# Decoder step: q, k and v of three token blocks in products of 512 columns, and modulation moved beside the RWKV inputs

## The chip, the core and the metric

The kernel runs on one core of a Trainium2 chip. The metric is the device time of one launch in microseconds, as a median over runs. TensorE multiplies, VectorE and ScalarE work on the elements, GpSimd does little here, and nearly all loads and stores are issued by SyncE, whose queue (SP) is taken in order.

## The reference

One layer of a decoder for a prompt of 2048 tokens and 64 sample tokens, all in fp32. Cut to what matters here:

```
sh1, sc1, gt1, sh2, sc2, gt2 = ada_modulation(c, w_ada, b_ada)   # silu(c) @ w_ada + b_ada, six parts of 1024
h = rms_norm(x, norm1_g) * (1.0 + sc1) + sh1
proj = h @ w_in                                                  # 1024 -> 3 * 512 (q, k, v) + 1792 (RWKV inputs P)
q, k = partial_rope(q), partial_rope(k)                          # 16 of each head's 64 elements turn
att = dilated attention of three branches over q, k, v
rw  = RWKV-7 time mixing over P (a recurrence over the tokens)
x = x + gt1 * (concat(att, rw) @ w_out)
h2 = rms_norm(x, norm2_g) * (1.0 + sc2) + sh2
x = x + gt2 * (square(relu(h2 @ w_ff1)) @ w_ff2)
y = rms_norm(x, normf_g)
```

k, v, the last row of P and the RWKV states are outputs too.

## The kernel before

The prompt is cut into four blocks of 512 tokens (0 to 3); block 3 also takes the 64 sample tokens. The tokens ORDER list the parts in the order in which they are written down, with a time span for each: i0 to i3 are the input projections (`in_stage`), r0 to r3 the RWKV recurrence, a0 to a3 the attention, s and c the sample tokens, m, p and f the output projection and the MLP. A scheduler then sets each engine's order from these times and its own costs, so parts overlap: RWKV of block 0 runs while blocks 0 to 2 are projected, and so on. All engines take their own list in order, so a row that waits holds back what stands behind it.

Every large product is done in three (`mm3`): operands are split into a high part and a rest (`split`: ScalarE writes the high part, VectorE the rest), and hi*hi, hi*lo and lo*hi are added in PSUM. `in_stage` of a block goes like this.

- For each of its token tiles (128 tokens; "tile 0" to "tile 3"): load x (name xt, two buffers), `norm_A` on ScalarE, then `norm_B`: eight transposes on TensorE in two groups of four (line 279, into PSUM tiles trps), eight scalings on VectorE (line 284, into h32, three buffers), split into hhi and hlo (lines 303, 304). hhi and hlo hold one block only, so these last two steps wait until the block before has been multiplied.
- Seven blocks of 256 weight columns for the RWKV inputs, block 6 first. Here the weights are stationary and the tokens stream, 512 columns a product (block 6 in two halves of 256 tokens). The result goes through pev to the DRAM scratch Pd.
- Six blocks of 256 weight columns for q, k and v. Here 128 tokens are stationary and 256 weight columns stream: 6 column blocks x 4 token tiles x 8 parts of the contraction x 3 = 576 products a block of tokens. Two token tiles share one PSUM bank; it is evicted by ScalarE (line 423, name qev, in two buffers of the tag pev), q and k are turned on VectorE, and the result goes to DRAM.

Weights come in two loads of 512 KB for each column block (name stg, two buffers), and the split halves go into w0 and w1 in turn. The modulation's parts 0 and 1 are made at the start. Parts 2 to 5 (`ada_rest`, a generator in S.bg) are made during block 1: before each of its 13 column blocks the generator takes three steps, a step being one load of 512 KB into stg and 32 small products (line 225) that add up in one PSUM bank.

PSUM has eight banks: two with the tag mm, for the large products; two with the tag tr, for the transposes of x and the modulation; four for RWKV and attention. Banks and buffers of a tag are handed out in the order in which the program is written.

Names in the rows: yps, zps, btps, vtps, aps, px, pu, psS, ops, lps are products and transposes of RWKV; qtps, s1ps, s2ps, ptps, pops of the attention; mps and wada the modulation.

Of the kernel before, what the change touches and what calls it, by code (L numbers as in the profile page):

```python
# [23 lines left out]
HD = 64  # L24
# [78 lines left out]
def run(gen, n):  # L103
    for _ in range(n):
        next(gen, None)
# [17 lines left out]
class Step:  # L123
# [184 lines left out]
        nc.scalar.activation(hi, h32[:, :, 0:rows], AF.Copy)  # L308
        nc.vector.tensor_tensor(lo, h32[:, :, 0:rows], hi.bitcast(F32), op=ALU.subtract)

    def mm3(self, out, wh, wl, xh, xl, nk):
        nc = self.nc
        self.tc.cur_priority += LEAD
        for k in range(nk):
            nc.tensor.matmul(out, wh(k), xh(k), start=k == 0, stop=False)  # L315
            nc.tensor.matmul(out, wh(k), xl(k), start=False, stop=False)  # L316
            nc.tensor.matmul(out, wl(k), xh(k), start=False, stop=k == nk - 1)  # L317
        self.tc.cur_priority -= LEAD

    def x_tile(self, j, X, norm=True):  # L320
# [6 lines left out]
    def w_in(self, c0, G):  # L327
        nc = self.nc
        tag = f"w{self.nwb % 2}"
        self.nwb += 1  # L330
        lo = G.tile([128, KD, 256], F32R, name="wlo", tag=tag)
        hi = G.tile([128, KD, 256], F32R, name="whi", tag=tag)
        for h in range(2):
            sl = slice(128 * h, 128 * h + 128)
            sg = G.tile([128, KD, 128], F32, name="stg", tag="stg")
            src = self.I["w_in"][0][:, c0 + 128 * h:c0 + 128 * h + 128]
            nc.sync.dma_start(sg, src.rearrange("(k p) c -> p k c", p=128))
            self.split(hi[:, :, sl], lo[:, :, sl], sg)
        return hi, lo

    def in_stage(self, s, G, psg, x0=(), first=None):
        nc, I, O = self.nc, self.I, self.O
# [26 lines left out]
            pend = new  # L369
        def wblock(c0):  # L370
            self.tick()
            w = first if first and c0 == 3 * ATT + 6 * 256 else self.w_in(c0, G)
            if self.bg is not None:
                run(self.bg, 3)
            return w

        for pb in (6, 0, 1, 2, 3, 4, 5):
            cols = self.halves(T) if last or pb == 6 else [(0, TS)]
            hi, lo = wblock(3 * ATT + pb * 256)
            evs = [G.tile([128, NW], F32, name="pev", tag="pev", bufs=2) for _ in range(2)]  # L380
            for c0, n in cols:
                for h in range(2):
# [19 lines left out]
        nc.sync.dma_start(rope[:, 0:4], I["rope"][t0:t0 + TS].rearrange("(j p) e -> p j e", p=128))  # L402
        if last:
            nc.sync.dma_start(rope[0:NS, 4], I["rope"][SEQ:SEQ + NS])
        for cb in range(6):
            hi, lo = wblock(cb * 256)
            kind, hh = cb // 2, (cb % 2) * 256
            for jp in range(3 if last else 2):
# [1077 lines left out]
def tile_hybrid_step(tc, I, O):  # L1486
# [76 lines left out]
    for tok in ORDER.split():  # L1563
# [5 lines left out]
        if tok[0] == "i":  # L1569
# [4 lines left out]
            if w == 0:  # L1574
                start.close()
                S.rwkv_setup()
                S.att_setup()
            if w == 1:
                full(S.bg)
                S.bg = None  # L1580
                S.A2, S.B2 = S.mod(3, 4, S.g2n, "A2")
# [111 lines left out]
```

## Time and profile before

| | |
|---|---|
| median of 3 runs | 3506.4 us (3504.91 to 3524.51) |
| the profiled execution | 3507.64 us, of which its span is 3505.8 us |
| TensorE busy | 3289.1 us, 94% of the span |
| weight loads of TensorE | 2794.4 us, 80% |
| VectorE, ScalarE busy | 2208.3 us (63%), 1709.7 us (49%) |
| mean granted TensorE clock | 0.965 |

A busy share counts a matmul from its start to the modelled end of its pipeline, so neighbours overlap, and a sum of matmul durations is more than the time they take. The time that a row of products needs is read from one start to the next. The profile has 40 slices of 87.6 us; the parts spoken of here lie in the first 960 us.

### The profile page before, as it was taken

The numbers are of one execution on the slowest core, as the hardware profiler recorded it, in microseconds if no ns is written. First come the engines' busy times: TensorE is split into PE (matmuls) and PEld (weight loads), VectorE is DVE, ScalarE is ACT, GpSimd is POOL, SyncE is SP. The second block draws the span as 40 slices with busy tenths as digits, with TensorE's granted clock in tenths as the row PEclk, the third lists the DMA queues.
The fourth block names the chain that finished last, engine by engine and source line by source line (L and its number), as shares of the span: only waits on it lengthen the run. The fifth ranks groups of instructions, "written<-read, shape, count | busy, mean of one in ns | idle before, by whom it ended". The sixth has DMA issues, their size and how long they took to land.

```text
span 3505.8 us, 66390 instructions
## 1 busy us (share of the span) xinstructions
PE 3289.1 (94%) x26546; PEld 2794.4 (80%) x26546; DVE 2208.3 (63%) x4872; ACT 1709.7 (49%) x3156; POOL 95.2 (3%) x219
## 2 busy tenths in 40 slices
PE   6999999888989999999999999799989998899998
PEld 4887888877878777878777777687767777899998
DVE  4565655625677566877766656675444877766666
ACT  4455444644355355546535442565333545544453
POOL 0000000000000000000000000000000000000000
PEclk8999999998989999999999999899999999899999
DMA  7456745434353443336344342843786335456564
GB/s 242 143 155 194 205 132 145 113 88 96 79 172 100 120 127 94 102 110 207 86 134 134 87 101 74 254 130 109 207 251 182 88 97 154 115 160 178 162 184 154
DMA packets 731757, 496.55 MB, mean 142 GB/s; under 512 B 126134, under 2 KB 682344, under 8 KB 731448
## 3 DMA queue, kind: packets, MB, share of 16 engines
q1 hardware_dynamic: 718824, 479.65, 47.6%
q0 software_dynamic: 12624, 12.65, 1.5%
q8 instruction: 210, 3.44, 0.4%
q14 instruction: 99, 0.81, 0.1%
HBM read 424.11 MB, written 63.77 MB: 139 GB/s over the span
## 4 chain that ended last, share of the span: by engine, by line
PE 79%; DMA 9%; ACT 5%; DVE 5%; issue 1%; SPq 0%; ACTq 0%; DVEq 0%
PE mmps L317 19%; PE mmps L315 19%; PE mmps L316 19%; PE pops L1047 2%; PE aps L652 2%; PE ptps L1057 2%; DMA out_dram<-pev 2%; DMA kst<-in_cache_k_dram 1%; DVE wl L259 1%; PE ktps L1231 1%; DMA stg<-in_w_out_dram 1%; DVE ql L951 1%; PE ops L794 1%; PE yps L729 1%; DMA wada<-in_w_ada_dram 1%
## 5 line engine op out<-in xcount | busy, mean ns | idle before, releaser
L258 ACT ACTIVATE wh<-stg 128x1024 fp32r<-128x1024 f32 x384 | 406.2, 1058 | 568.8 <-PE mmps L316 473.8
L315 PE MATMUL mmps<-h2hi,wh 128*128 128x256 f32 (+2 forms) x1864 | 628.4, 337 | 13.1 <-ACT h2hi L303 7.9
L317 PE MATMUL mmps<-h2hi,wl 128*128 128x256 f32 (+2 forms) x1864 | 628.7, 338 | 9.5 <-DVE wl L259 9.4
L259 DVE TENSOR_TENSOR wl<-stg,wh 128x1024 fp32r<-128x1024 f32 x384 | 469.9, 1225 | 260.3 <-ACT wh L258 240.9
L316 PE MATMUL mmps<-h2lo,wh 128*128 128x256 f32 (+2 forms) x1864 | 627.6, 337 | 1.0 <-DVE h2lo L304 1.0
L315 PE MATMUL mmps<-hid,wh 128*128 128x512 f32 (+2 forms) x1280 | 460.2, 361 | 5.6 <-ACT rlu L1419 3.8
L317 PE MATMUL mmps<-hid,wl 128*128 128x512 f32 (+2 forms) x1280 | 461.6, 361 | 0.1
L316 PE MATMUL mmps<-hid,wh 128*128 128x512 f32 (+2 forms) x1280 | 460.8, 360 | 0.0
L315 PEld LDWEIGHTS mmps<-h2hi,wh 128*128 128x128 f32 x1864 | 360.7, 194 | 44.5 <-ACT h2hi L303 8.8
L317 PEld LDWEIGHTS mmps<-h2hi,wl 128*128 128x128 f32 x1864 | 359.7, 193 | 41.2 <-DVE wl L259 12.0
L316 PEld LDWEIGHTS mmps<-h2lo,wh 128*128 128x128 f32 x1864 | 360.5, 193 | 30.0 <-issue 1.8
L315 PEld LDWEIGHTS mmps<-hid,wh 128*128 128x128 f32 x1280 | 243.5, 190 | 36.6 <-ACT rlu L1419 4.3
L317 PEld LDWEIGHTS mmps<-hid,wl 128*128 128x128 f32 x1280 | 243.7, 191 | 31.9 <-issue 3.4
L316 PEld LDWEIGHTS mmps<-hid,wh 128*128 128x128 f32 x1280 | 243.9, 191 | 29.4 <-issue 1.8
L1302 DVE SCALAR_TENSOR_TENSOR acc<-mmps,ada,acc 128x512 f32<-128x512 f32 (+1 forms) x280 | 179.3, 642 | 129.8 <-PE mmps L317 128.7
L315 PE MATMUL mmps<-whi,hhi 128*128 128x256 f32 (+1 forms) x816 | 233.8, 286 | 0.0
L317 PE MATMUL mmps<-whi,hlo 128*128 128x256 f32 (+1 forms) x816 | 233.1, 286 | 0.0
L316 PE MATMUL mmps<-wlo,hhi 128*128 128x256 f32 (+1 forms) x816 | 233.0, 286 | 0.0
L315 PE MATMUL mmps<-hhi,whi 128*128 128x512 f32 (+2 forms) x608 | 213.4, 353 | 13.5 <-ACT pev L393 6.9
L316 PE MATMUL mmps<-hlo,whi 128*128 128x512 f32 (+2 forms) x608 | 212.2, 350 | 1.1 <-DVE hlo L304 1.1
L317 PE MATMUL mmps<-hhi,wlo 128*128 128x512 f32 (+2 forms) x608 | 211.9, 349 | 0.0
L259 DVE TENSOR_TENSOR wlo<-stg,whi 128x1024 fp32r<-128x1024 f32 x104 | 126.6, 1228 | 90.9 <-ACT whi L258 90.5
(345 smaller groups left out, 5886.8 us busy)
## 6 DMA issues: line engine op xcount, KB each, us to landing
stg<-in_w_ff_dram SPq DMA_DIRECT2D x320, 512.0 KB
stg<-in_w_in_dram SPq DMA_DIRECT2D x104, 512.0 KB
stg<-in_w_out_dram SPq DMA_DIRECT2D x64, 512.0 KB
kst<-in_cache_k_dram SPq DMA_DIRECT2D x80, 256.0 KB
vst<-in_cache_v_dram SPq DMA_DIRECT2D x80, 256.0 KB
xt<-in_x_prompt_dram SPq DMA_DIRECT2D x32, 512.0 KB
wada<-in_w_ada_dram SPq DMA_DIRECT2D x32, 512.0 KB
Pd<-pev SPq DMA_DIRECT2D x56, 256.0 KB
```

Of the source, the lines that this page charges most:

```text
L258: nc.scalar.activation(hi, src, AF.Copy)
L259: nc.vector.tensor_tensor(lo, src, hi.bitcast(F32), op=ALU.subtract)
L315: nc.tensor.matmul(out, wh(k), xh(k), start=k == 0, stop=False)
L316: nc.tensor.matmul(out, wh(k), xl(k), start=False, stop=False)
L317: nc.tensor.matmul(out, wl(k), xh(k), start=False, stop=k == nk - 1)
L652: nc.tensor.matmul(pt[:, hp], bk[o:o + 64, hp, c], F[o:o + 64, hp, c], start=True, stop=True)
L729: nc.tensor.matmul(pz[q, u], x, y, start=True, stop=True, tile_position=(64 + o, 64 + o))
L794: nc.tensor.matmul(po[o:o + 64, h // 2, 64 * c:64 * c + 64], UV[0:64, c, h], AO[:, unit(h)], start=False, stop=c == 1 and h >= 6, tile_pos ...
L951: nc.vector.tensor_tensor(lo, pv[o], hi.bitcast(F32), op=ALU.subtract)
L1047: nc.tensor.matmul(out[o:o + 64], v[:, o:o + 64], pT[:, j], start=j0 + j < 2, stop=j0 + j >= len(jobs) - 2, tile_position=(0, o),)
L1057: nc.tensor.transpose(pt[:, j], jb[j][0], self.ident)
L1302: nc.vector.scalar_tensor_tensor(o, pt[:, 0:np_], gt[:, ob, 0:1], o, op0=ALU.mult, op1=ALU.add)
```

## The change

For blocks 0 to 2 the six column blocks of q, k and v are replaced by `qkv_rows`, called once each for q, k and v. It takes all 512 columns of its kind at once, and the contraction in two halves of 512 rows. For each half it makes two loads of 512 KB (now rows of 2 KB instead of 512 B), splits them, and multiplies for four token tiles: 4 parts x 3 products with 512 streaming columns, 2 halves x 4 tiles x 12 = 96 products a kind, 288 a block of tokens instead of 576. The sums of the four token tiles stay open in four PSUM banks at once, two of the tag mm and two of the tag tr, and are evicted one after another in the second half. One eviction still has 512 columns. The rotation is done for 64 elements a row at once, so in 6 instead of 12 instructions an eviction.

Since the tr banks are taken there, the modulation's steps can no longer stand beside q, k and v: the generator is now run before the RWKV column blocks of blocks 1 and 2 (three steps before column blocks 6, 0, 1, 2 and two before 3, 4, 5, so 18 in each), and its end, with the second norm's factors, moves from after block 1 to after block 2. Block 3 and all that follows are as before.

```diff
-    def mm3(self, out, wh, wl, xh, xl, nk):
+    def mm3(self, out, wh, wl, xh, xl, nk, start=True, stop=True):
...
+    def qkv_rows(self, kind, t0, hhi, hlo, rope, G, psg):
+
+        nc, I, O = self.nc, self.I, self.O
+        csl = slice(ATT * kind, ATT * kind + ATT)
+        dst = (self.qd, O["k_win"][0, 0].rearrange("t h e -> t (h e)"), O["v_win"][0, 0].rearrange("t h e -> t (h e)"))[kind]
+        pts = [psg.tile([128, 512], F32, name="mmps", tag="mm" if j < 2 else "tr") for j in range(4)]
+        for kh in range(2):
+            self.tick()
+            tag = f"w{self.nwb % 2}"
+            self.nwb += 1
+            lo = G.tile([128, 4, ATT], F32R, name="wlo", tag=tag)
+            hi = G.tile([128, 4, ATT], F32R, name="whi", tag=tag)
+            for i in range(2):
+                sg = G.tile([128, 2, ATT], F32, name="stg", tag="stg")
+                r0 = 512 * kh + 256 * i
+                nc.sync.dma_start(sg, I["w_in"][0][r0:r0 + 256, csl].rearrange("(k p) c -> p k c", p=128))
+                sl = slice(2 * i, 2 * i + 2)
+                self.split(hi[:, sl], lo[:, sl], sg)
+            for j in range(4):
+                tok = slice(128 * j, 128 * j + 128)
+                self.mm3(
+                    pts[j],
+                    lambda k: hhi[:, 4 * kh + k, tok],
+                    lambda k: hlo[:, 4 * kh + k, tok],
+                    lambda k: hi[:, k],
+                    lambda k: lo[:, k],
+                    4, kh == 0, kh == 1,
+                )
+                if kh == 0:
+                    continue
+                ev = G.tile([128, ATT], F32, name="qev", tag="pev", bufs=2)
+                nc.scalar.activation(ev, pts[j], AF.Copy, scale=-0.125 if kind == 0 else 1.0)
...
+                nc.sync.dma_start(dst[t0 + 128 * j:t0 + 128 * j + 128], ev)
...
-            w = first if first and c0 == 3 * ATT + 6 * 256 else self.w_in(c0, G)
-            if self.bg is not None:
-                run(self.bg, 3)
-            return w
+            return first if first and c0 == 3 * ATT + 6 * 256 else self.w_in(c0, G)
...
             hi, lo = wblock(3 * ATT + pb * 256)
+            if self.bg is not None:
+                run(self.bg, 2 if pb in (3, 4, 5) else 3)
...
-        for cb in range(6):
+        if not last:
+            for kind in range(3):
+                self.qkv_rows(kind, t0, hhi, hlo, rope, G, psg)
+        for cb in range(6 if last else 0):
...
-            if w == 1:
+            if w == 2:
                 full(S.bg)
                 S.bg = None
```

From the last products of a0 and the first column blocks of i3 on, the engines' lists read alike before and after. The places below lie ahead of that. Line numbers after line 339 are higher in the changed kernel.

TensorE before, from the last q, k and v products of block 0 (mmps_1595) into the first products of block 1 (mmps_4810, mmps_4836); hhi_247 and hhi_4653 are the two blocks' tokens:

```order
L316 MATMUL mmps_1595<-wlo_1533,hhi_247 128x256
L317 MATMUL mmps_1595<-whi_1534,hlo_248 128x256
L639 MATMUL btps_2299<-ident_90,bk_2119 128x64 x8
L639 MATMUL btps_2309<-ident_90,bk_2119 128x64 x8
L315 MATMUL mmps_4810<-hhi_4653,whi_4780 128x256
L315 MATMUL mmps_4836<-hhi_4653,whi_4780 128x256
L316 MATMUL mmps_4810<-hlo_4654,whi_4780 128x256
L317 MATMUL mmps_4810<-hhi_4653,wlo_4779 128x256
L315 MATMUL mmps_4810<-hhi_4653,whi_4780 128x256
```

TensorE after, at the same place: the last product of block 0, and then transposes of block 1's x (xt_4319 is its tile 0, xt_4327 its tile 1) among RWKV's rows:

```order
L317 MATMUL mmps_1182<-whi_1242,hlo_248 128x512
L687 MATMUL btps_1963<-ident_90,bk_1783 128x64 x8
L687 MATMUL btps_1973<-ident_90,bk_1783 128x64 x4
L279 MATMUL trps_4347<-ident_90,xt_4319 128x128 x4
L687 MATMUL btps_1973<-ident_90,bk_1783 128x64
L279 MATMUL trps_4367<-ident_90,xt_4327 128x128 x4
L687 MATMUL btps_1973<-ident_90,bk_1783 128x64 x3
L787 MATMUL zps_1670<-sol_1551,AT_1471 32x32 x16
```

TensorE after, a little further on, behind eleven more rows of aps and px (xt_4358 is tile 2 of block 1):

```order
L700 MATMUL aps_1997<-F_1782,bk_1783 128x128
L279 MATMUL trps_4378<-ident_90,xt_4327 128x128 x4
L279 MATMUL trps_4398<-ident_90,xt_4358 128x128 x4
L315 MATMUL mmps_4474<-hhi_4317,whi_4444 128x256
L315 MATMUL mmps_4500<-hhi_4317,whi_4444 128x256
L316 MATMUL mmps_4474<-hlo_4318,whi_4444 128x256
L317 MATMUL mmps_4474<-hhi_4317,wlo_4443 128x256
```

Before, no transposes of x stand at this place. Now seven of block 1's eight groups of four stand behind the last product of block 0, and tile 2's first group stands ahead of block 1's first product.

SyncE's queue before, while block 0's RWKV inputs are made (xt_4655, 4663, 4694 and 4725 are block 1's four tiles):

```order
L364 DMA xt_4655<-in_x_prompt_dram 128x1024
L364 DMA xt_4663<-in_x_prompt_dram 128x1024
L402 DMA rope_5422<-in_rope_dram 128x4x16
L364 DMA xt_4694<-in_x_prompt_dram 128x1024
L337 DMA stg_529<-in_w_in_dram 128x8x128
L396 DMA Pd_65<-pev_353 128x512
L337 DMA stg_533<-in_w_in_dram 128x8x128
L396 DMA Pd_65<-pev_354 128x512
L364 DMA xt_4725<-in_x_prompt_dram 128x1024
```

SyncE's queue after, around the stores of block 0's v (qev_1293, qev_1308; xt_4358 and xt_4389 are block 1's tiles 2 and 3, xt_8556 and xt_8564 block 2's tiles 0 and 1, stg_4582 and stg_4586 the weights of block 1's second column block):

```order
L385 DMA out_3_dram<-qev_1293 128x512
L545 DMA raw_2237<-Pd_65 128x4x129
L545 DMA raw_2275<-Pd_65 128x4x129
L385 DMA out_3_dram<-qev_1308 128x512
L410 DMA xt_4358<-in_x_prompt_dram 128x1024
L410 DMA xt_4389<-in_x_prompt_dram 128x1024
L410 DMA xt_8556<-in_x_prompt_dram 128x1024
L410 DMA xt_8564<-in_x_prompt_dram 128x1024
L213 DMA wada_4466<-in_w_ada_dram 128x1024
L337 DMA stg_4582<-in_w_in_dram 128x8x128
L337 DMA stg_4586<-in_w_in_dram 128x8x128
```

The loads of tiles 2 and 3 have moved from among block 0's RWKV inputs to behind block 0's v, and four loads of x now stand in one row ahead of modulation's and the weights' next loads.

## Rows read from the trace of the kernel before

**Rows 1.** The page of the profile: part 1 (busy time of each engine, share of the span, instructions) and the line PEclk of part 2 (granted TensorE clock in tenths of full speed, 40 equal slices of the span).

```profile
PE 3289.1 (94%) x26546; PEld 2794.4 (80%) x26546; DVE 2208.3 (63%) x4872; ACT 1709.7 (49%) x3156; POOL 95.2 (3%) x219
...
PEclk8999999998989999999999999899999999899999
```

**Rows 2.** Busy time by stretch of the first 832 us. Columns: start and end of the stretch in us, its length, busy us of TensorE (PE, with the count of instructions), its weight loads (PEld), VectorE, ScalarE, GpSimd, then the granted clock, the DMA share and GB/s. 45 to 219 is the input projection of token block 0, 219 to 443 that of block 1, 443 to 658 that of block 2; 139 to 219, 351 to 443 and 560 to 658 hold the q, k and v of blocks 0, 1 and 2, and 658 to 832 the first part of block 3.

```profile
139.00:219.00 80.00, 79.69 (x683) 77.58 (x681) 57.83 (x209) 42.15 (x80) 5.44 (x13) 1.00 0.52 150
219.00:351.00 132.00, 130.51 (x1330) 98.48 (x1330) 76.16 (x168) 69.67 (x134) 7.94 (x18) 1.00 0.61 177
351.00:443.00 92.00, 91.09 (x830) 82.75 (x831) 56.92 (x209) 37.31 (x60) 2.20 (x6) 1.00 0.71 204
...
560.00:658.00 98.00, 91.90 (x831) 87.70 (x831) 65.65 (x225) 53.86 (x100) 0.00 (x0) 1.00 0.55 159
658.00:832.00 174.00, 142.23 (x1114) 129.44 (x1111) 74.46 (x191) 81.60 (x204) 4.41 (x11) 0.93 0.43 91
```

**Rows 3.** Matmuls by form, over the whole span. Columns: line, engine, operation, tiles (out<-moving,stationary), shapes, count | busy us, mean ns of one | idle us before them.

```profile
L315 PE MATMUL mmps<-whi,hhi 128*128 128x256 f32 x768 | 220.1, 287 | 0.0
...
L315 PE MATMUL mmps<-hhi,whi 128*128 128x512 f32 x288 | 115.4, 401 | 0.0
```

**Rows 4.** Timeline of TensorE at the end of block 0's last products with 256 columns: start in us, duration in us, instruction. The rows left out are 30 more products of the same form, so that there are 31 steps from the first to the last.

```profile
213.80 0.28 PE L316 MATMUL mmps<-wlo,hhi 128*128 128x256 f32 x1
...
217.52 0.28 PE L317 MATMUL mmps<-whi,hlo 128*128 128x256 f32 x1
```

**Rows 5.** The same view in block 0's RWKV inputs, products with 512 columns. There are 15 steps from the first row to the second and 38 from the second to the third.

```profile
99.69 0.39 PE L317 MATMUL mmps<-hhi,wlo 128*128 128x512 f32 x1
...
103.17 0.40 PE L317 MATMUL mmps<-hhi,wlo 128*128 128x512 f32 x1
...
111.80 0.39 PE L316 MATMUL mmps<-hlo,whi 128*128 128x512 f32 x1
```

**Rows 6.** Who TensorE waited for, 220 to 443 us. Columns: the waiting instruction <- the one it waited for: us in total, times, longest.

```profile
PE mmps L315 <- ACT hhi L303: 1.3, 1, 1.3
PE mps L225 <- DMA wada<-in_w_ada_dram: 0.5, 1, 0.5
```

**Rows 7.** The same view, 660 to 830 us.

```profile
PE ptps L1057 <- ACT s L1031: 11.5, 4, 7.1
PE mmps L315 <- ACT pev L393: 6.9, 3, 3.1
```

**Rows 8.** Timeline from block 0's last product to block 1's first ones and a little beyond (TensorE alone; in brackets the idle time of the engine before the row and what ended it).

```profile
217.73 1.02 PE L639 MATMUL btps<-ident,bk 64*128 64x64 f32 x16
220.09 0.51 PE L315 MATMUL mmps<-hhi,whi 128*128 128x256 f32 x2 [1.34 <-ACT hhi L303]
220.98 0.39 PE L316 MATMUL mmps<-hlo,whi 128*128 128x256 f32 x1 [0.39 <-DVE hlo L304]
...
222.50 0.60 PE L644 MATMUL vtps<-ident,mv 128*64 128x128 f32 x4
223.04 1.16 PE L652 MATMUL aps<-F,bk 64*128 64x128 f32 x8
```

**Rows 9.** The transposes of x (tile trps) by form in two stretches, 50 to 220 us and 450 to 657 us. Columns: count, shortest/median/longest ns, first and last start in us.

```profile
L279 PE MATMUL trps<-ident,xt x40: 270/272/472, 51.9 to 86.0; 128*128 128x128 f32 x40
...
L279 PE MATMUL trps<-ident,xt x32: 270/272/331, 452.7 to 476.0; 128*128 128x128 f32 x32
```

**Rows 10.** What VectorE does to one half of a token tile after its transposes, by form, 443 to 560 us (columns as in rows 3).

```profile
L284 DVE TENSOR_SCALAR h<-trps,A,ada 128x128 f32<-128x128 f32 x32 | 10.8, 404 | 5.0 <-PE trps L279 5.0
...
L304 DVE TENSOR_TENSOR hlo<-h,hhi 128x512 fp32r<-128x512 f32 x8 | 5.2, 689 | 4.9 <-ACT hhi L303 4.9
```

**Rows 11.** Timeline of one x tile of block 2, from the issue of its load to the last step of its norm (the copies and other rows between left out).

```profile
421.64 0.35 SPq L364 DMA_DIRECT2D xt<-in_x_prompt_dram  x1
...
426.68 1.06 ACT L266 ACTIVATE sqj<-xt 128x1024 bf16<-128x1024 f32 x1 [1.60 <-DMA xt<-in_x_prompt_dram]
...
428.42 1.15 ACT L269 ACTIVATE xt<-xt,st 128x1024 f32<-128x1024 f32 x1
```

**Rows 12.** Pieces of the chain of waits, 219 to 443 us: start us, us, what.

```profile
237.60 1.12 PE zps L739 x32
239.87 1.12 PE zps L743 x32
```

**Rows 13.** The last block's second norm (MLP, line 279 again), where two token tiles are normed with little else on the engines: the stretch 3222 to 3236 us (columns as in rows 2).

```profile
3222.00:3236.00 14.00, 10.36 (x67) 9.21 (x67) 11.79 (x29) 8.46 (x14) 0.00 (x0) 0.91 0.12 40
```

**Rows 14.** Timeline of the same stretch: the first transposes, the last split of the second tile and TensorE's waits around it.

```profile
3223.01 1.03 PE L279 MATMUL trps<-ident,xt 128*128 128x128 f32 x8
...
3232.58 0.38 PE L315 MATMUL mmps<-hid,wh 128*128 128x320 f32 x1 [1.56 <-DVE h L284]
...
3233.15 0.68 DVE L304 TENSOR_TENSOR h2lo<-h,h2hi 128x512 fp32r<-128x512 f32 x1
...
3234.82 0.64 PE L315 MATMUL mmps<-hid,wh 128*128 128x320 f32 x1 [1.71 <-ACT rlu L1419]
```

**Rows 15.** Modulation's products, the evictions of q, k and v and the products of the rotation, by form, 139 to 560 us (columns as in rows 3).

```profile
L225 PE MATMUL mps<-wada,cT 128*32 128x256 f32 x256 | 21.8, 389 | 0.6 <-DMA wada<-in_w_ada_dram 0.5
...
L435 DVE TENSOR_TENSOR rt<-qev,rope 128x32 f32<-128x32 f32 x128 | 15.1, 189 | 17.6 <-ACT qev L423 17.6
...
L423 ACT ACTIVATE qev<-mmps 128x512 f32<-128x512 f32 x24 | 14.2, 592 | 37.9 <-PE mmps L317 27.2 <-issue 10.7
```

More of the change, by code (lines that the diff above doesn't have):

```diff
@@ L314, in mm3 @@
         for k in range(nk):
-            nc.tensor.matmul(out, wh(k), xh(k), start=k == 0, stop=False)
+            nc.tensor.matmul(out, wh(k), xh(k), start=start and k == 0, stop=False)
             nc.tensor.matmul(out, wh(k), xl(k), start=False, stop=False)
-            nc.tensor.matmul(out, wl(k), xh(k), start=False, stop=k == nk - 1)
+            nc.tensor.matmul(out, wl(k), xh(k), start=False, stop=stop and k == nk - 1)
         self.tc.cur_priority -= LEAD
@@ L339, in w_in @@
         return hi, lo
+    def qkv_rows(self, kind, t0, hhi, hlo, rope, G, psg):
[29 more added lines that the diff above has]
+                nc.scalar.activation(ev, pts[j], AF.Copy, scale=-0.125 if kind == 0 else 1.0)
+                if kind < 2:
+                    a = ev.rearrange("p (h e) -> p h e", e=HD)
+                    sh = [128, 8, 8]
+                    cosb = rope[:, j, None, 0:8].to_broadcast(sh)
+                    sinb = rope[:, j, None, 8:16].to_broadcast(sh)
+                    rt = G.tile([128, 4, 64], F32, name="rt", tag="rt", bufs=2)
+                    r = [rt[:, i].rearrange("p (h e) -> p h e", e=8) for i in range(4)]
+                    t1, t2 = a[:, :, 0:8], a[:, :, 8:16]
+                    for i, (x, c) in enumerate(((t1, cosb), (t2, sinb), (t1, sinb), (t2, cosb))):
+                        nc.vector.tensor_tensor(r[i], x, c, op=ALU.mult)
+                    nc.vector.tensor_tensor(t1, r[0], r[1], op=ALU.subtract)
+                    nc.vector.tensor_tensor(t2, r[2], r[3], op=ALU.add)
+                nc.sync.dma_start(dst[t0 + 128 * j:t0 + 128 * j + 128], ev)
```

## The prediction

> **What bounds the kernel now.** I read the page first: TensorE is busy 94% of the span at a clock that is near full in nearly all slices [rows 1]. So the first question is what TensorE does in the stretches that the change touches. The table by stretch answers it: from 139 to 443 us TensorE is busy 99% of the time at a granted clock of 1.00 (2.4 GHz), with q, k and v as with the RWKV inputs and modulation; from 560 to 658 us it is still 94%; from 658 us, in block 3, it drops to 82% [rows 2]. The waits say the same: between 220 and 443 us TensorE waited 1.3 us once for hhi and 0.5 us for modulation's weights, and hardly for anything else [rows 6]. Only in block 3, which is not rewritten, do waits of some length stand (11.5 us and 6.9 us, [rows 7]). Blocks 0 to 2 are bound by TensorE's own work, and a gain there must come from fewer or shorter steps of TensorE; whatever is saved on VectorE, ScalarE or in the loads has no wait to remove.
>
> From the end of a0 on the lists of all engines are the same in both kernels. So what is gained or lost by about 700 us is carried to the end; I look for no second effect there.
>
> **The wide products.** The mean durations mislead here: 287 ns for a product with 256 columns, 401 ns with 512 [rows 3]. Two narrow ones for one wide one would save 173 ns, 149 us over 864 pairs. But neighbours overlap, so I take start to start. 256 columns: (217.52 - 213.80) / 31 = 0.120 us [rows 4]. 512 columns: (111.80 - 103.17) / 38 = 0.227 us, and a slower piece just before, (103.17 - 99.69) / 15 = 0.232 us [rows 5]. A pair saves 2 x 0.120 - 0.227 = 0.013 us or, by the slower piece, 0.008 us. The change replaces 3 x 576 = 1728 narrow products by 864 wide ones: 864 x 0.013 = 11 us, or 864 x 0.008 = 7 us. I take 9 us, all of it on the path, since TensorE is the bound there.
>
> The Trainium skill (TensorE: Matmul & The Clock Gate, Back-to-back issue gap) gives about 131 ns for a 512-column product in a sustained stream with weight loads. By that a pair would save 109 ns and the change 94 us; the trace does not agree, since such a stream takes 227 ns a product here [rows 5].
>
> **The four banks.** This is the new cost. Before, block 1's transposes of x ran at 60 to 86 us, far ahead, and all of block 3's first ones at 453 to 476 us [rows 9]; at the border TensorE had only to wait for hhi and hlo, 1.34 + 0.39 = 1.7 us after 1.0 us of btps [rows 8]. Now the tr banks carry q, k and v until the end of v, so nearly all transposes of the next block come behind its last product. Call that moment T, and follow what the first products of block 1 wait for. Their row stands behind tile 2's first transposes. Tile 2's x can be loaded only when tile 0 has left its buffer, after tile 0's second transposes, which need the bank of the last token tile (one eviction, 0.59 us [rows 15]): T + 1.4 us. The load takes 426.68 - 421.64 = 5.0 us and the norm 428.42 + 1.15 - 426.68 = 2.9 us [rows 11], so the transposes and the first product come at about T + 10 us. Meanwhile VectorE must do four half tiles at 4 x 0.404 + 0.689 = 2.3 us [rows 10], 9.2 us, which ends at about the same time. What TensorE has in between: btps 1.0, vtps 0.6, aps 1.2 [rows 8], two zps at 1.1 [rows 12] and twenty transposes at 1.03 us for eight [rows 14], with px about 8 us, all work that before stood elsewhere. So 2 us idle up to the first product. Then tile 3: its buffer is free only after tile 1's second transposes, about T + 8 us, plus 7.9 us for load and norm, T + 16; TensorE has 35 narrow products (4.2 us) and is there at about T + 14.7, idle 1.3 us. The second half of column block 6 then waits for tile 3's splits, some 1.5 us. Idle 4.8 us against 1.7 us before, 3 us more.
>
> Two smaller pieces come on top. SyncE's row of four loads ends only after tile 3's transposes, and the weights of the second column block stand behind it: 0 to 3 us, I take 1. And idle TensorE costs clock: in the last norm of the MLP, where the same chain is bare, two tiles took 3223.0 to 3233.8 us [rows 14], TensorE was busy 10.4 of 14 us, and the granted clock was 0.91 [rows 13], so 0.5 us again. Together 4.5 us a border. The nearest row for the whole is that stretch, 3.6 us idle and 1.3 us of clock in 14 us, 4.9 us against the border's old 1.7. At the third border RWKV offers less to fill with and the sample tile adds a load, but block 3 already waits there; I take the same. Three borders: 13.5 us; bounds 2 us each (filled by RWKV) and 10 us each (every load late): 6 to 30 us.
>
> **What costs nothing.** Modulation's products, 21.8 us busy in block 1 [rows 15], move by half into block 2; TensorE is full in both, so they cost there what they cost here, give or take 3 us. Their loads and waits on SyncE move with them, out of the q, k and v of block 1, where TensorE waited 0.5 us for them. The rotation's instructions halve, 3 x 48 fewer at 0.189 us [rows 15], 27 us of VectorE; VectorE was busy 60 to 72% there and nobody's last wait, so 0, at best 3 us. The evictions are 12 a block as before, but now four in a row at 2.7 us (12 x 0.227), with two qev buffers that each wait for their store. The stores' time shows in no row above; against the spacing of 5.8 us before, the third and fourth may hold ScalarE some 2 us each for q and k. What comes next needs those banks only 8 us later, and the wait is covered by the next kind's first products. If that cover fails, 2 us for each q and k, 12 us in all; I take 0 and keep 12 for the range.
>
> **The sum.** 3507.6 (the profiled execution, 1.8 us around its span) - 9 + 13.5 = 3512 us; that execution lies 1.2 us above the median of the runs, so 3511 us, 0.1% above before. A measurement of this kernel tells a change from none at about 1%, 35 us.
>
> **Rivals.** *Borders filled.* RWKV's rows behind v and the first narrow products may cover all of the chain, since the scheduler has put them there. Then the extra is 2 us a border: 3506.4 - 9 + 6 = 3503 us, with the other small gains 3497. For it speaks that VectorE's chain and the load overlap; against it that tile 2's load is bare whatever fills it, 7.9 us of load and norm.
>
> *The queue of loads decides, slower.* SyncE takes its list in order. At each border the third and fourth loads of x wait until tiles 2 and 3 are transposed; behind them stand modulation's loads, the weights of the next column block, and RWKV's dA stores that start its solve. If tile 3 comes at T + 25 rather than T + 16, the weights land so late that a column block of 11 us stands still, and RWKV's products, which TensorE takes in order, come late too: about 14 us a border, 42 in all, with the evictions' 6 us of their 12, less 9: 3545 us. It decides from the fourth load of a row issued more than 25 us behind the last v product. Against it: before, modulation's loads and Pd's stores also stood ahead of dA, and TensorE did not wait.
>
> *Wide products are much cheaper in a full stream.* By the busy times a pair saves 0.17 us, 149 us, so 3371 us with the borders. By the 131 ns of the Trainium skill (the page and section named above) it would be 94 us, 3426 us. Against it stand 53 steps in a row at 0.227 to 0.232 us [rows 5]: this kernel has such products already, and they take that.
>
> **Chances and range.** The forecast 0.52, borders filled 0.28, the queue 0.14, cheaper products 0.04, other 0.02. The first two lie within 1%, as does a little of the third: the same 0.81, faster by over 1% 0.06, slower 0.13. The range goes from full gain and filled borders, 3506 - 11 - 3 + 6 less a few us for what moves in the order, 3488, to 3506 - 7 + 30 + 12, 3541.
>
> **What would show it.** Right: in the q, k and v of blocks 0 to 2, 288 products a block, 0.227 to 0.232 us from start to start, so that the three stretches shrink by some 3 us each; at each border the first transposes of x just behind v, the first product about 10 us behind the last, and TensorE idle 4 to 6 us, with waits for h, hhi or the norm where only hhi stood; the clock a little below 1.00 there; from a0's end on the same times, shifted by one amount. Wrong: products under 0.2 us; waits of TensorE for weights (wlo) or for qev's banks inside q, k and v; borders without idle time; or a shift that grows or shrinks after 700 us, which would mean that the same order does not keep the same time.

## The result, and the profile after

The change makes the kernel slower by two thirds of a per cent: a ratio of 1.0066, 95% interval 1.0050 to 1.0082, medians 3539.2 against 3519.2 us (13 executions each; the 3506.4 us above was the median of three). That lies within the 1% of the likeliest case and within the range; but the forecast was 4.5 us more, and it became 23 (0.0066 x 3519). Where the other 18 come from is the question of what follows.

The page of after, as [rows 1]:

```profile
PE 3307.8 (94%) x25682; PEld 2763.5 (78%) x25682; DVE 2203.4 (62%) x4728; ACT 1712.5 (48%) x3156; POOL 95.1 (3%) x219
...
PEclk8999999998979999999999999999999989999999
```

TensorE has 864 rows fewer and is busy 19 us longer, in a span of 3532.2 us instead of 3505.8. The stretches of [rows 2], after (443 to 560 was not shown before; there the clock had been 1.00):

```profile
139.00:219.00 80.00, 80.00 (x522) 63.36 (x521) 57.55 (x168) 43.30 (x84) 5.76 (x13) 1.00 0.52 154
219.00:351.00 132.00, 126.35 (x1156) 94.55 (x1157) 75.98 (x173) 68.94 (x127) 7.96 (x18) 0.97 0.58 171
351.00:443.00 92.00, 92.00 (x674) 73.57 (x673) 53.47 (x156) 37.68 (x65) 2.39 (x10) 1.00 0.42 127
443.00:560.00 117.00, 111.51 (x980) 82.96 (x979) 56.53 (x126) 46.86 (x80) 3.11 (x3) 0.96 0.57 169
```

The q, k and v stretches (139 to 219, 351 to 443) are full, at full clock. The loss stands in the two stretches that begin at a border.

**The shift stays.** The same product of RWKV in both kernels, with its first and last start, before and then after:

```profile
L837 PE MATMUL gps<-sgl,r_g x136: 270/275/475, 267.3 to 3113.2; 128*128 128x128 f32 x128, 128*128 128x64 f32 x8
```

```profile
L885 PE MATMUL gps<-sgl,r_g x136: 270/275/474, 269.7 to 3139.5; 128*128 128x128 f32 x128, 128*128 128x64 f32 x8
```

In block 1 the shift is 2.4 us, at the end 26.3. By landmarks between: 24.5 us at 732 us, 22.4 at 979, 26.9 at 1100 and then 27 to within a few us until the end. So nearly all of it is there at 732 us, before a0 ends (its last product starts at 762.7 us before and 788.6 us after). Behind that the order is the same, and the shift moves a little where the clock differs: it grows by 4.5 us over a stretch in which TensorE has the same 1077 rows in both (before, then after; columns as in [rows 2]):

```profile
979.00:1100.00 121.00, 112.06 (x1077) 102.17 (x1074) 91.61 (x195) 74.50 (x137) 5.10 (x12) 0.91 0.50 144
```

```profile
1001.40:1126.90 125.50, 116.42 (x1077) 105.94 (x1074) 91.72 (x195) 74.53 (x137) 5.09 (x12) 0.87 0.48 139
```

**The borders.** From the start of the last product of a block to that of the first of the next it takes 11.2, 7.3 and 8.9 us, where it took 2.6, 2.4 and 2.5 (the expectations below say 11.1 for the first). The first border, TensorE alone, as [rows 8]:

```profile
217.00 0.40 PE L317 MATMUL mmps<-whi,hlo 128*128 128x512 f32 x1
217.33 0.77 PE L687 MATMUL btps<-ident,bk 64*128 64x64 f32 x12
218.09 0.66 PE L279 MATMUL trps<-ident,xt 128*128 128x128 f32 x4
...
227.65 0.66 PE L279 MATMUL trps<-ident,xt 128*128 128x128 f32 x4 [1.63 <-ACT xt L269]
228.19 0.50 PE L315 MATMUL mmps<-hhi,whi 128*128 128x256 f32 x2
...
237.53 0.60 PE L279 MATMUL trps<-ident,xt 128*128 128x128 f32 x4
240.76 1.07 PE L225 MATMUL mps<-wada,cT 128*32 128x256 f32 x16 [2.64 <-DVE h L284]
```

T is 217.0. Tile 2's norm releases its transposes at T + 10.6, and the first product starts at T + 11.2: as the chain of the prediction had it (T + 10). Most of these 11 us are filled with rows of RWKV. What was not foreseen is the last row: modulation's first products need a tr bank, and stand behind the last transposes of x, whose bank VectorE still empties. They wait 2.64 us here and 2.64 at the second border.

What TensorE waited for in after, 40 to 982 us (columns as in [rows 6]):

```profile
PE trps L279 <- ACT xt L269: 8.8, 3, 6.6
...
PE mps L225 <- DVE h L284: 5.3, 2, 2.6
...
PE trps L279 <- DVE h L284: 3.9, 2, 2.4
...
PE mps L225 <- DMA wada<-in_w_ada_dram: 2.2, 2, 1.9
```

The 6.6 is the start of the kernel, in both. The other waits are new, but for 0.5 us each that before waited for the norm and for modulation's weights. The clock behind the borders differs too. Stretches that begin at the three borders (columns as in [rows 2]), before:

```profile
217.50:260.00 42.50, 40.77 (x567) 32.74 (x566) 25.40 (x50) 22.26 (x44) 3.87 (x6) 1.00 0.48 135
441.80:490.00 48.20, 47.62 (x515) 40.50 (x514) 30.52 (x62) 29.09 (x53) 1.12 (x5) 1.00 0.47 143
657.00:700.00 43.00, 37.39 (x315) 33.11 (x313) 27.94 (x85) 25.64 (x59) 0.00 (x0) 0.96 0.35 87
```

And after:

```profile
217.00:260.00 43.00, 37.79 (x400) 30.66 (x400) 27.08 (x59) 24.23 (x45) 1.98 (x5) 0.92 0.44 141
443.00:490.00 47.00, 43.40 (x367) 34.15 (x366) 31.33 (x69) 26.47 (x49) 2.07 (x2) 0.93 0.50 151
674.00:717.00 43.00, 33.40 (x246) 30.09 (x245) 27.68 (x93) 21.16 (x40) 0.00 (x0) 0.84 0.30 89
```

Idle (length less busy): 1.7, 0.6 and 5.6 us before, 5.2, 3.6 and 9.6 after, 10.5 us more. Clock (busy time by the missing share): 37.39 x 0.04 = 1.5 us before, 37.79 x 0.08 + 43.40 x 0.07 + 33.40 x 0.16 = 11.4 after, 10 us more.

**The ledger.** From one start on TensorE to the next, all time from block 0's first product to block 3's last is either idle, or lost to the clock, or belongs to the row that runs. Before this takes 912.7 us, after 934.5:

| us | before | after | difference |
|---|---|---|---|
| products of q, k and v | 303.8 | 297.6 | -6.2 |
| products of the RWKV inputs | 343.0 | 341.4 | -1.6 |
| transposes of x | 11.2 | 13.7 | +2.5 |
| modulation | 19.7 | 21.1 | +1.4 |
| RWKV and attention | 167.0 | 169.6 | +2.6 |
| idle | 51.2 | 62.6 | +11.4 |
| lost to the clock | 16.7 | 28.4 | +11.7 |

One profile could mislead, since the clock differs from run to run. But each execution comes with its span and mean granted clock, so span x (1 - clock) is what it lost to the clock, and the rest is work and idle time at full clock. In the mean of 95 executions of before and 22 of after:

| | mean time | lost to the clock | rest of the span |
|---|---|---|---|
| before | 3518.3 | 131.5 | 3384.8 |
| after | 3541.1 | 142.1 | 3397.2 |
| difference | +22.8 | +10.6 | +12.4 |

By this table nearly half of the loss is clock. But the two columns are not independent: a straight line through the 95 executions of before says that one with 1 us more lost to the clock is only 0.75 us longer. By that slope the 10.6 us of clock cost some 8 of the 22.8 us, and a longer loss to the clock makes the rest look shorter. The ledger is rougher still: by the same count the second profile of after, taken later, has some 9 us more idle time, much of it one wait of 8.3 us in block 3.

### The profile page after: what moved, and what is told of

It reads as the page before. It is cut to its first block, busy times and chain, and to the rows that moved or that the text cites. A ratio compares the mean times of both kernels' runs of the same rounds, so it can differ in the third digit from the quotient of the medians.

```text
span 3532.2 us, 64529 instructions
## 1 busy us (share of the span) xinstructions
PE 3307.8 (94%) x25682; PEld 2763.5 (78%) x25682; DVE 2203.4 (62%) x4728; ACT 1712.5 (48%) x3156; POOL 95.1 (3%) x219
## 4 chain that ended last, share of the span: by engine, by line
PE 79%; DMA 10%; ACT 5%; DVE 4%; issue 2%; SPq 0%; ACTq 0%; DVEq 0%
PE mmps L317 19%; PE mmps L315 19%; PE mmps L316 19%; PE pops L1095 2%; PE aps L700 2%; PE ptps L1105 2%; DMA kst<-in_cache_k_dram 1%; DMA out_dram<-pev 1%; DMA stg<-in_w_out_dram 1%; DMA wada<-in_w_ada_dram 1%; PE ktps L1279 1%; DVE wl L259 1%; DMA stg<-in_w_ff_dram 1%; DMA stg<-in_w_in_dram 1%; PE ops L842 1%
## 5 line engine op out<-in xcount | busy, mean ns | idle before, releaser
L315 PE MATMUL mmps<-hhi,whi 128*128 128x512 f32 (+2 forms) x608 | 218.6, 363 | 13.7 <-ACT pev L438 6.9
L315 PE MATMUL mmps<-whi,hhi 128*128 128x512 f32 (+2 forms) x528 | 184.2, 349 | 0.0
L316 PE MATMUL mmps<-wlo,hhi 128*128 128x512 f32 (+2 forms) x528 | 184.0, 349 | 0.0
L317 PE MATMUL mmps<-whi,hlo 128*128 128x512 f32 (+2 forms) x528 | 183.5, 348 | 0.0
```

What stands on the lines that cost most here:

```text
L315: nc.tensor.matmul(out, wh(k), xh(k), start=start and k == 0, stop=False)
L317: nc.tensor.matmul(out, wl(k), xh(k), start=False, stop=stop and k == nk - 1)
```

## The experiments

All ratios are against the kernel before, on the same chip. "Gaps" are those at the three borders in the profile, from start to start; the last two columns are differences from before in the means over all executions, as in the table above. One execution scatters by 9 us in what it loses to the clock, so a mean of 12 is good to some 3 us, one of 6 to 4.

| kernel | ratio, 95% interval | gaps, us | clock | rest |
|---|---|---|---|---|
| after | 1.0066, 1.0050 to 1.0082 | 11.2, 7.3, 8.9 | +10.6 | +12.4 |
| two_banks | 1.0003, 0.9984 to 1.0022 | 2.9, 1.8, 2.6 | +2.5 | -0.3 |
| v_two | 1.0023, 1.0002 to 1.0045 | 2.4, 2.4, 3.4 | +13.0 | -5.3 |
| pairs_02 | 1.0024, 1.0009 to 1.0039 | 2.9, 3.1, 5.0 | +6.9 | +2.1 |
| wide_b0 | 1.0028, 1.0012 to 1.0045 | 11.2, 3.1, 2.5 | +7.3 | +4.3 |
| tr_first | 1.0035, 1.0013 to 1.0058 | 2.8, 2.4, 2.7 | +9.5 | +4.8 |
| mod_alone | 1.0003, 0.9989 to 1.0017 | 2.6, 2.4, 2.5 | +7.4 | -7.4 |
| two_banks_mod | 1.0034, 1.0022 to 1.0045 | 2.9, 2.4, 5.0 | +4.8 | +5.9 |
| mod_late | 1.0057, 1.0037 to 1.0078 | 10.9, 10.2, 8.7 | +9.9 | +9.3 |
| mod_later | 1.0098, 1.0074 to 1.0123 | 10.9, 10.2, 8.7 | +20.1 | +16.6 |

### Give the banks back: two_banks, v_two

```diff
-        pts = [psg.tile([128, 512], F32, name="mmps", tag="mm" if j < 2 else "tr") for j in range(4)]
-        for kh in range(2):
...
+        ws = []
+        for jp in range(2):
+          self.tick()
+          pts = {j: psg.tile([128, 512], F32, name="mmps", tag="mm") for j in (2 * jp, 2 * jp + 1)}
+          for kh in range(2):
...
-            for j in range(4):
+            for j in (2 * jp, 2 * jp + 1):
```

> The wide products of the changed kernel, but only two token tiles at a time, in the two mm banks; the weights of both halves of the contraction stay in w0 and w1 for the two pairs of tiles. The tr banks are free again, so the next block's x can be transposed ahead, as before the change. Modulation stands beside the RWKV inputs of blocks 1 and 2, as in the changed kernel. Theory A (the four banks cost the time, at the borders between the blocks): the three gaps from the last product of a block to the first of the next fall from 11.1, 7.3 and 8.9 us to the old 2.5, the clock stays at 1.00 there, and what is left is the gain of the wide products: 5 to 10 us faster than the kernel before, near 0.998 of its time. Theory B (the halved contraction and the bunched evictions cost it, or the wide products gain nothing): the gaps close, and the time is still 5 to 20 us above before, 1.002 to 1.006. A third way: with weights kept for two passes the split of the next half comes late, TensorE waits for wlo in each of q, k and v, 1 to 3 us nine times, and the time is 0 to 20 us above before.

Measured: 1.0003. The first border again, two_banks:

```profile
224.32 0.40 PE L317 MATMUL mmps<-whi,hlo 128*128 128x512 f32 x1
...
226.32 0.96 PE L692 MATMUL btps<-ident,bk 64*128 64x64 f32 x15
227.21 0.51 PE L315 MATMUL mmps<-hhi,whi 128*128 128x256 f32 x2
```

No transposes of x stand there, and TensorE does not wait at this border. With the same wide products, the same halves and modulation in its new place, the ratio falls from 1.0066 to 1.0003. So the loss goes when the tr banks are given back. That is not the banks alone: the edit also changes the order of the products and lets evictions come two at a time instead of four; v_two and tr_first, below, change less. The gain of 5 to 10 us did not come, though: in this profile's ledger q, k and v take 6.3 us less, but TensorE waits 4.6 us for modulation's weights, of which 3.7 in block 1:

```profile
PE mps L225 <- DMA wada<-in_w_ada_dram: 3.7, 4, 1.7
```

v_two keeps four banks for q and k, and takes v in pairs (`qkv_pairs`, not shown, is the loop of two_banks):

```diff
...
-                self.qkv_rows(kind, t0, hhi, hlo, rope, G, psg)
+                (self.qkv_rows if kind < 2 else self.qkv_pairs)(kind, t0, hhi, hlo, rope, G, psg)
```

> The changed kernel with q and k in four banks as it has them, but v two token tiles at a time in the two mm banks, so that the tr banks are free from the end of k on, some 27 us before the block's last product. Theory A (what costs is that the tr banks are held up to the very end of a block, so that the next x is transposed only behind it): the gaps at the three borders fall to 2 to 4 us, the clock is 1.00 there, modulation waits for no bank, and the time is that of the kernel with two banks throughout, 0 to 5 us above the kernel before, ratio 0.999 to 1.002. Rival (four banks cost wherever they are held, by evictions in a bunch or products in another order): at least half of the changed kernel's loss stays, 10 us and more above before, 1.003 and more.

Measured: 1.0023, between the two, and the interval reaches into the ranges of both. The gaps close as theory A says, and without the clock it is 5.3 us better than before: four banks cost no time outside the clock while they are held in the middle of a block. But it loses 13 us of clock, as much as the changed kernel, and theory A had no such loss. Its profile, the two stretches where block 1 and block 2 begin:

```profile
217.00:223.00 6.00, 4.07 (x19) 3.86 (x20) 5.61 (x12) 4.17 (x9) 0.00 (x0) 0.72 0.85 254
...
436.00:442.00 6.00, 5.52 (x115) 4.84 (x108) 5.01 (x11) 5.18 (x12) 0.00 (x0) 0.67 0.56 167
```

A gap of 2.4 us, with 1.9 us idle or less, and the clock falls behind it. In the profile of [rows 2] such gaps went by at 1.00 at the first two borders.

### One border: wide_b0

```diff
-        if not last:
+        wide = s == 0
+        if wide:
             for kind in range(3):
...
-        for cb in range(6 if last else 0):
+        for cb in range(0 if wide else 6):
```

Modulation is back beside all of block 1.

> The kernel before with the change in block 0 alone: its q, k and v wide and in four banks, blocks 1 and 2 narrow, modulation where it was, beside all of block 1. So there is one border of the new kind, the first. Theory A: that border costs what it does in the changed kernel, a first product 11 us behind the last instead of 2.5, then the wait of modulation for its bank (2.6 us) and 3 us of clock, less 2 us for the products of block 0: 8 to 12 us above the kernel before, 1.002 to 1.0035, some 0.4 of the whole loss. Rival (the loss is not at the borders, but grows with the wide products and modulation's place): under 4 us above, 1.000 to 1.001, with RWKV's rows moved from block 1 to the border making up for it.

Measured: 1.0028, 10 us, as theory A had it. One border of the new kind costs 0.4 of the whole loss, with modulation in its old place.

### The chain: tr_first

```diff
-        pts = [psg.tile([128, 512], F32, name="mmps", tag="mm" if j < 2 else "tr") for j in range(4)]
+        pts = [psg.tile([128, 512], F32, name="mmps", tag="tr" if j < 2 else "mm") for j in range(4)]
```

> The changed kernel with the four banks handed out the other way round: the first two token tiles in the tr banks, the last two in the mm banks. In the second half of v the tr banks are then evicted first, some 5.5 us (24 products of 0.229) before the block's last product, and the next block's first transposes, the second loads of x and their norms can start that much earlier. Nothing else changes. Theory A (the chain of transposes, load and norm behind the tr banks sets the border): the gaps from the last product of a block to the first of the next fall from 11.1, 7.3 and 8.9 us by 3 to 5 us each, and the time falls by 8 to 15 us against the changed kernel, to 1.002 to 1.0045 of the kernel before. Rival (a border is set by what RWKV, modulation and VectorE have to do there, not by when the banks come free): gaps shrink by less than 2 us, and the time is within 4 us of the changed kernel's.

Measured: 1.0035, half of the loss gone, within the range that theory A gave. The gaps do not shrink by 3 to 5 us but close altogether (2.8, 2.4 and 2.7 us), since all that hangs on the tr banks moves ahead with them:

```profile
218.67 0.39 PE L317 MATMUL mmps<-whi,hlo 128*128 128x512 f32 x1
218.99 0.90 PE L687 MATMUL btps<-ident,bk 64*128 64x64 f32 x14
219.81 0.66 PE L279 MATMUL trps<-ident,xt 128*128 128x128 f32 x4
220.40 0.34 PE L687 MATMUL btps<-ident,bk 64*128 64x64 f32 x2
221.43 0.51 PE L315 MATMUL mmps<-hhi,whi 128*128 128x256 f32 x2 [0.69 <-ACT hhi L303]
222.32 0.38 PE L316 MATMUL mmps<-hlo,whi 128*128 128x256 f32 x1 [0.39 <-DVE hlo L304]
```

Of what is left two thirds is clock, +9.5 us in the mean against +4.8 for the rest. In the profiled execution it was much more clock. TensorE from 216 to 282 us in pieces of 6 us:

```profile
222.00:228.00 6.00, 5.43 (x19) 4.03 (x19) 3.55 (x10) 4.43 (x10) 0.00 (x0) 0.56 0.30 89
228.00:234.00 6.00, 6.00 (x17) 4.18 (x17) 0.98 (x3) 0.00 (x0) 0.00 (x0) 0.50 0.01 3
...
240.00:246.00 6.00, 4.52 (x44) 3.52 (x43) 3.11 (x8) 4.22 (x9) 0.00 (x0) 1.00 0.55 157
...
252.00:258.00 6.00, 6.00 (x61) 5.26 (x62) 1.24 (x2) 2.90 (x4) 0.94 (x4) 0.50 0.31 87
258.00:264.00 6.00, 6.00 (x41) 5.33 (x40) 3.49 (x6) 0.78 (x2) 0.00 (x0) 0.50 0.28 90
...
276.00:282.00 6.00, 6.00 (x69) 3.94 (x68) 3.63 (x9) 3.54 (x7) 1.04 (x1) 1.00 0.44 110
```

### Modulation: mod_alone, two_banks_mod, mod_late, mod_later

mod_alone is the kernel before with the generator's steps moved as in the change, and nothing else.

> The kernel before with one part of the change alone: modulation's steps moved from all 13 column blocks of block 1 to the RWKV column blocks of blocks 1 and 2; q, k and v in the old narrow products. Theory A (the move costs nothing by itself, since TensorE is full in both blocks and the x transposes stay ahead): 0 to 2 us above the kernel before, ratio 1.000 to 1.0006. Theory C (the place beside the RWKV inputs is what costs, by modulation's weights that come late or by longer transitions): 8 to 20 us above, 1.002 to 1.006.

Measured: 1.0003. The move costs nothing in sum, as theory A had it. In the means the rest is 7.4 us shorter and the clock takes 7.4 us more, with gaps as before; why is not shown.

two_banks_mod is two_banks with three steps before each of block 1's 13 column blocks or halves, as before the change.

> As the two-bank kernel, and modulation back in its old place, three steps before each of the 13 column blocks or halves of block 1. So this is the wide products alone, against the kernel before. Theory A: 5 to 10 us faster than the kernel before, and within 3 us of the two-bank kernel with modulation moved. Theory C (modulation's place costs): faster than that one by 5 us and more.

Measured: 1.0034, a miss for theory A and the opposite of what theory C asks. Wide products with modulation among them take 11 to 12 us more than before, though no tr bank is held to a block's end. In this profile TensorE waited in block 1 (224 to 462 us):

```profile
PE mps L225 <- DMA wada<-in_w_ada_dram: 3.5, 3, 1.6
PE mmps L315 <- ACT whi L258: 1.8, 1, 1.8
```

That would be about half. But two_banks waited 4.6 us for the same weights and lost nothing, so these waits do not tell the two apart, and the cause stays open.

The next two leave modulation out at the first column blocks of the changed kernel, mod_late at block 6:

```diff
-                run(self.bg, 2 if pb in (3, 4, 5) else 3)
+                run(self.bg, 0 if pb == 6 else 3)
```

mod_later at blocks 6 and 0, the first two (it has steps before 1 to 5, so also before the last; its expectation puts that wrongly):

```diff
-                run(self.bg, 2 if pb in (3, 4, 5) else 3)
+                run(self.bg, {1: 4, 2: 4, 3: 4, 4: 3, 5: 3}.get(pb, 0))
```

> The changed kernel, but modulation's generator is not run before column block 6, the first of a block of tokens; it takes three steps before each of the six others, again 18 a block. In the changed kernel modulation's first product stands right behind the last transposes of x and waits 2.6 us for their tr bank, at the first and at the second border, and the granted clock falls behind that wait. Theory A (this wait is one of the costs of the borders): both waits go, with some 1.5 us of clock each, 4 to 8 us below the changed kernel, so 14 to 20 us above the kernel before. Rival: the chain of loads and norms stands behind it anyway and the next products wait for hhi instead: within 2 us of the changed kernel.

Measured: 1.0057, the changed kernel's time within the interval. The edit did not do what it was meant to: the scheduler has set modulation's products right behind the transposes of x again, and both waits of 2.6 us are there. So it does not decide between the two.

> The changed kernel, but modulation takes no step before the first two column blocks and the last of a block of tokens, and 4, 4, 4, 3 and 3 steps before the others but these. The kernel that left out only the first column block still had modulation's first products right behind the last transposes of x, waiting 2.6 us for their bank, and took the changed kernel's time, so it told nothing. Here they stand a column block later, when the bank is long free. Theory A (this wait is part of the loss): the waits of modulation for the bank are gone at the first and the second border, 2.6 us each with some 1.5 us of clock each, and the time is 5 to 8 us below the changed kernel, 1.004 to 1.005 of the kernel before. Rival (the products behind would wait for hhi anyway): no gain, within 2 us of the changed kernel, 1.006 to 1.007.

Measured: 1.0098, slower still by 0.3%, which neither had expected. The waits for the bank are gone. In their place, at the first border (215 to 265 us):

```profile
PE mmps L315 <- ACT hhi L303: 3.7, 1, 3.7
PE trps L279 <- ACT xt L269: 3.3, 1, 3.3
```

So the rival is right about the mechanism: behind modulation stand products that wait for tile 3's hhi, 3.7 us instead of 2.6. And the clock is lower for longer behind it:

```profile
238.00:244.00 6.00, 4.21 (x29) 3.76 (x30) 5.41 (x12) 4.93 (x9) 0.00 (x0) 0.51 0.14 57
244.00:250.00 6.00, 6.00 (x68) 5.54 (x65) 1.68 (x4) 1.18 (x2) 0.40 (x2) 0.50 0.01 3
...
256.00:262.00 6.00, 6.00 (x47) 5.17 (x46) 2.72 (x6) 1.14 (x3) 0.00 (x0) 0.50 0.06 8
```

### A version to keep: pairs_02

Here blocks 0 and 2 take q, k and v in pairs of token tiles, and block 1 is narrow with modulation beside it.

> A version meant to keep what is good: blocks 0 and 2 have q, k and v wide, two token tiles at a time in the mm banks, block 1 is narrow with modulation beside it as in the kernel before. No tr bank is held, no product of modulation stands beside wide ones. Theory A (the wide products save some 2 us a block where nothing else is disturbed): 2 to 5 us below the kernel before, 0.9986 to 0.9994, at the edge of what can be measured. Rival (weights split for two passes and longer transitions to RWKV's rows eat it): 0 to 6 us above, 1.000 to 1.002.

Measured: 1.0024, on the rival's side and a little beyond its range. No version beats the kernel before.

### The same kernels again

> The kernel before, unchanged, for a second profile and as a control of the measurement. In the profile the prediction rests on, the granted clock was 1.00 all the way from 139 to 657 us, with a gap of 2.5 us at each border. The kernel with modulation moved alone had the same gaps and stretches at half clock behind them. If the clock at a border depends on how the idle time happens to fall, this profile has one or two stretches at half clock behind borders, and block 3 begins up to 5 us later than 659.4 us. If not, 1.00 again and 659 us. Ratio 1.000 within 0.0015 either way.

> The changed kernel, unchanged, for a second profile beside the others. Gaps at the three borders again 11.1, 7.3 and 8.9 us within 0.5 us, modulation's two waits for its bank again 2.6 us, since they follow from the engines' lists; the stretches at half clock behind them in other places or of other length, 25 to 40 us in all between 139 and 720 us. Ratio 1.0066 within 0.0015.

Before again: 0.9991, 0.9970 to 1.0011, and gaps of 2.6, 2.4 and 2.5 us. At the first border, 218.8 to 261 us, the clock was 0.96 this time, and block 3 began at 664.5 us, where it was 659.6:

```profile
218.80:261.00 42.20, 40.61 (x560) 32.65 (x559) 23.69 (x45) 21.80 (x43) 2.67 (x6) 0.96 0.46 128
```

After again: 1.0075, 1.0048 to 1.0102, gaps 11.2, 7.3 and 9.0 us, modulation's two waits 2.6 us each, clock 0.92, 0.96 and 0.84 behind the borders, and some 27 us at half clock between 139 and 720 us. So the gaps and modulation's waits follow from the order and repeat to a tenth; the clock behind them moves by up to 0.04.

## Why the prediction was off

**Right: what bounds the kernel and what happens later.** Blocks 0 to 2 are TensorE's, 24.5 us of the shift are there before a0 ends, and it is carried on within a few us.

**Right in kind, too large: the wide products.** A piece of block 0's q in after:

```profile
139.65 0.40 PE L315 MATMUL mmps<-whi,hhi 128*128 128x512 f32 x1
...
145.71 0.40 PE L317 MATMUL mmps<-whi,hlo 128*128 128x512 f32 x1
146.04 1.01 PE L687 MATMUL btps<-ident,bk 64*128 64x64 f32 x16
```

There are 26 steps between the first two, 0.233 us each. 6.2 us were saved instead of 9. Over the steps of blocks 0 to 2 that no other row disturbs, the mean is 0.1192 us for a narrow product and 0.2305 us for a wide one, so a pair saves 0.008 us and 864 pairs some 7 us: the slower piece of [rows 5] was the one to take. A row of another kind can start later than the next product would, 0.33 us behind a wide one (145.71 to 146.04) instead of 0.23, 0.21 us behind a narrow one ([rows 4, 8]) instead of 0.12; that is 0.1 us at both widths, and takes only some 0.5 us of the gain. The mean duration of 400 ns would have misled, as supposed. The Trainium skill's 131 ns (TensorE: Matmul & The Clock Gate, Back-to-back issue gap) does not hold in this stream either. The check on the length of the stretches was ill chosen: from first product to last block 0's is 1.3 us longer, block 1's 7.2 us and block 2's 1.1 us shorter, since RWKV's and modulation's rows move between stretches.

**Right in the sum, in part by luck: the idle time at the borders, 10.5 us against 9.** Up to the first product the chain came as worked out, 1.6 us idle at the first border against 2. Behind it the sum had 1.3 us for tile 3 and 1.5 us for its splits; 0.5 us for hhi and 2.6 us for modulation's bank came instead. So 5.3 us of the 10.5 are modulation's waits for its bank, which I had not followed: I moved modulation past the q, k and v where its bank is taken, to the place where the x transposes now take the same bank, and counted it as nothing. mod_later shows that hhi stands next behind it, with 3.7 us where I had 1.5, so that this time could not be had back by moving modulation once more.

**Wrong: the clock, 0.5 us a border.** This is the step that failed. It was taken from one stretch of 14 us at 0.91 [rows 13], and the clock there was measured over that stretch alone. Even that row gives more, 1.3 us by the prediction's own count (14 us at 0.91), and no reason was given for taking less. Behind the borders half clock lasted beyond the idle time, into products that run without a wait: 3.0, 3.0 and 3.8 us more in the profile, 10.6 us in the mean of all executions, against 1.5 in the sum. The profile before showed 1.00 from 139 to 658 us, past the first two borders; the second profile showed 0.96 behind the first of them. Why the clock falls as far as it does stays open: two_banks, with closed gaps, loses 2.5 us of it, and v_two, with closed gaps too, 13.

**Too small: what I costed at nothing.** Transposes of x in eight pieces among other rows, modulation, RWKV and attention take 6.5 us more in the ledger, the RWKV inputs 1.6 less; against them stands 1 us a border for SyncE's row of loads. 8.5 for the clock, 3 for the products, 1.5 for idle time and 2 for the rest make 15 of the 18 us that are missing; the ledger is of one profile, and no better than that.

**The rivals.** The queue of loads did not decide: its condition was a fourth load more than 25 us behind the last v product, and the row that holds it ends 21.5 us behind (T = 217.0):

```profile
218.78 19.74 SPq L410 DMA_DIRECT2D xt<-in_x_prompt_dram  x4
241.47 0.33 SPq L213 DMA_DIRECT2D wada<-in_w_ada_dram  x1
```

The borders were not filled, and the products not cheaper. The evictions cost what was taken, 0 of up to 12 us: TensorE waited 0.5 us for qev in all, though ScalarE waited 3.9 us for stores.

## What to carry to other kernels

A buffer that carries work ahead across a border was worth more here than the products that it could speed up: before PSUM banks are lent to another use, list every row that takes them next, and count what comes behind the last use of each. Where TensorE is full, idle time at a border can cost more than itself: here 10.5 us of it came with some 10 us of clock. That is no rule, since mod_alone, v_two and tr_first lost 7 to 13 us of clock with gaps of 2.4 to 3.4 us. If a border must be, hand out first the banks that the next stage needs first; swapping two tags did that here and took away half of the loss.

## What was not expected of the hardware

The granted clock stayed at 0.50 (1.2 GHz) while TensorE was busy without a break: 6.00 of 6 us in each piece from 252 to 264 us of tr_first, and from 244 to 262 us of mod_later, in tr_first behind 1.5 us of idle time (240 to 246 us), in mod_later behind the wait of 3.7 us; the kernel before did work of the same kinds at 1.00. At that level products with 256 columns start every 0.21 us (in after, at 229.28, 229.49 and 229.70 us) instead of 0.12. The same gap of 2.6 us left the clock at 1.00 in one profile of the kernel before and took it to 0.96 over the next 42 us in the other. What decides between these, and why mod_alone, v_two and tr_first lose 7 to 13 us of clock with closed gaps where two_banks loses 2.5, the runs do not settle.
